# Ten column orders for the moving weights of the second MLP matrix, put back by VectorE

## The chip, the cores and the metric

One core of one Trainium2 chip runs the whole program. The metric is the device time of that core in microseconds (us), from the first to the last instruction of one execution; the lower the better. Two timed runs of the kernel before took 2423.46 and 2424.36 us, median 2423.91 us.

## The reference, cut to what matters

The program is one decoder layer over 512 tokens with a model width of 2048. What the change touches is the last matrix product, the second matrix of a squared-ReLU MLP with a hidden width of 8192:

```python
h = rmsnorm(x, g_mlp[l])
u = jnp.square(jax.nn.relu(jnp.einsum('bsd,df->bsf', h, w_ff1[l])))
x = x + jnp.einsum('bsf,fd->bsd', u, w_ff2[l])
return rmsnorm(x, g_final)
```

Here `u` is 512 x 8192, `w_ff2` is 8192 x 2048 and the result is 512 x 2048, all float32.

## The kernel before, in words

Every large product of the program is done by a scheme with seven block products in place of eight (Strassen's, in Winograd's form: A11, A12, S1 to S4, A22 name the seven left operands), and each float32 operand is split into a high and a low part of a rounded float32 format (`th` and `tl` on the weight side). A block product is then three matmuls for each slice of 128 of the inner dimension: high times high (line 187), high times low of the left operand (line 189), and the low part of the weights (line 191). ScalarE makes the high part (`high_of`, line 111), VectorE the low part (`low_of`, line 114).

The second MLP matrix is the loop at the end of the program. It runs over 8 segments of 1024 hidden columns (`seg`) and, in each, over two halves of 1024 output columns (`cg`): 16 **units**, each a call of `unit(seg, cg, ST)`. A unit loads four weight tiles `y` of 128 x 4 x 512 (line 1600, from the SP queue), forms three sums of them on VectorE (line 128), and runs its products through `run`, which splits the weights and calls `mm_rows`. There the stationary operand is a 128 x 128 piece of the left operand (`us`), and **the moving operand is a row slice `hi[:, q, :]` or `lo[:, q, :]` of the weights, 512 columns wide**, read from the first column to the last. One product is 2 row blocks x 12 matmuls of 512 columns. A unit has seven: four go to the PSUM accumulator `a` (A11, S2, S1, S4), two to the second accumulator `d` (S3, A22), one to `b` (A12).

After most products `into(i, j, ps)` adds the accumulator, two blocks of 128 x 512, onto the result rows `x` in SBUF: in the first segment ScalarE copies (line 1617), later VectorE adds (`add`, line 131), and where the residual has already been added to the rows (`in_rows`), VectorE multiplies by a factor for each row and adds (`onto_rows`, line 1535). The function `residual` (line 1578) puts one of the four places into `in_rows` at the end of each unit of segments 3 to 6: (0, 0), (1, 0), (1, 1), (0, 1) in that order. S3 goes to place (1, 1), A22 to place (1, 0).

The order of the work on each engine follows from the program's order and a scheduler that may move instructions; `a` and `d` swap their two PSUM bank pairs from unit to unit, so the `d` of one unit is the `a` of the next.

Of the kernel before, what the change touches and what calls it, by code (L numbers as in the profile page):

```python
# [11 lines left out]
AF = mybir.ActivationFunctionType  # L12
ALU = mybir.AluOpType
# [32 lines left out]
def tile_hybrid_block(ctx: ExitStack, tc, x, g_mix, w_in, b_f, b_gate, conv_w, w_conv_out,  # L46
                      w_attn_out, w_mix_out, g_mlp, w_ff1, w_ff2, g_final, out):
    nc = tc.nc
    x, out = x[0], out[0]
# [13 lines left out]
    def bank(i, name):  # L63
        return psum.tile([P, S], F32, tag=f"p{i}", name=name)
# [39 lines left out]
    def tied(i):  # L104

        if strict[0]:
            tc.keep_in_program_order(i)
        return i
# [7 lines left out]
    def split(src, hi, lo):  # L116
        return high_of(src, hi), low_of(src, hi, lo)
# [12 lines left out]
    def add(out, a, b):  # L130
        return nc.vector.tensor_tensor(out=out, in0=a, in1=b, op=ALU.add)
# [39 lines left out]
                    else:  # L171
                        nc.tensor.matmul(o, lo[:, q, js], Sh, start=False, stop=q == nq - 1, skip_group_check=True)  # L172

    def mm_rows(ps, Sx, hi, lo, first, extra=None, blocks=range(2), qs=None):

        nq, w = hi.shape[1], hi.shape[2]
        for b in blocks:
            o = ps[b][:, :w] if len(ps) == 2 else ps[0][:, b * w:(b + 1) * w]
            begin = first and (b == 0 or len(ps) == 2)
            ts = slice(b * P, (b + 1) * P)  # L180
            for part in range(2):
                for q in qs or range(nq):
                    Sh, Sl = (e[:, ts] for e in Sx(q))
                    if extra == "first" and part == 0 and q == 0 and b == 0:
                        nc.tensor.matmul(o[:, :192], Sh, hi[:, q, :192], start=True, stop=False, skip_group_check=True)
                    if part == 0:
                        tied(nc.tensor.matmul(o, Sh, hi[:, q, :], start=begin and q == 0, stop=False,  # L187
                                              skip_group_check=True))
                        tied(nc.tensor.matmul(o, Sl, hi[:, q, :], start=False, stop=False, skip_group_check=True))  # L189
                    else:  # L190
                        tied(nc.tensor.matmul(o, Sh, lo[:, q, :], start=False, stop=q == nq - 1,  # L191
                                              skip_group_check=True))

    def mm_late(ps, Sx, hi, lo, first):
# [331 lines left out]
    class Quarters:  # L526
# [28 lines left out]
        def turn(self, t, par, banks):  # L555

            out = []
            for n, i in enumerate(banks):
                pt = bank(i, "ptr").rearrange("p (k s) -> p k s", k=4)
                for k in range(4):  # L560
                    c = 2 * (4 * n + k) + par
                    tied(nc.tensor.matmul(pt[:, k, :], xin[t][:, c * P:(c + 1) * P], dgs[t], start=True, stop=True))
                out.append(pt)
            return out
# [147 lines left out]
    awake, pv = bank(3, "awake"), bank(7, "pv")  # L712
# [27 lines left out]
    a, b = (gV0.acc(k)[0] for k in "ab")  # L740
# [5 lines left out]
    pv = bank(2, "pv")  # L746
# [93 lines left out]
    for t in range(NT):  # L840
# [3 lines left out]
                            op0=ALU.mult)  # L844
# [51 lines left out]
    begin = {(q, k): const.tile([P, 1], F32, name=f"begin{q}{k}") for q in range(CT // 2) for k in range(3)}  # L896
    for b in begin.values():
        nc.vector.memset(b, 1.0)
    seen = const.tile([P, 1], F32, name="seen")
# [45 lines left out]
    def apart(i, name="S4", row=4):  # L945

        spare = bank(i, "spare")

        def extra(q, Sh, h):
            if q == row:  # L950
                nc.tensor.matmul(spare[:, :192], h[:, :P], Sh[:, :192], start=True, stop=True)
        return {name: extra}
# [17 lines left out]
    n = 0  # L970
    for g in (4, 2, 0, 5, 3, 1):
# [8 lines left out]
        if n == NH // 2:  # L980
# [5 lines left out]
                    extra={} if n < NH // 2 else {"A11": "first", **apart(4, "S2", 0)}))  # L986
# [3 lines left out]
    for f in range(0, KT, 2):  # L990
# [7 lines left out]
        if n == 4 + CT:  # L998
# [5 lines left out]
            for i, raw in enumerate(araw):  # L1004
# [3 lines left out]
                    extra=apart(4, "S2", 0)))  # L1008
# [46 lines left out]
    class Products:  # L1055
# [9 lines left out]
        def place(self, k, units):  # L1065
            self.tile(main.tile([P, 4, 2, 2, HS], F32R, tag=f"t{k}", name="M"), units)
# [157 lines left out]
    n = turns[0] + 1  # L1224
# [174 lines left out]
    common, turned = const.tile([P, 1], F32, name="common"), const.tile([P, NT], F32, name="turned")  # L1399
# [127 lines left out]
    in_rows = set()  # L1527
# [54 lines left out]
    def banks2(i, name):  # L1582
        return tuple(pairs.tile([P, S], F32, tag=f"q{i}{e}", name=name) for e in range(2))

    def unit(seg, cg, ST):

        a, d = banks2(cg, "a"), banks2(1 - cg, "d")
        if seg == 0:  # L1590
            kept[cg] = banks2(2 + cg, "b")
        b = kept[cg]
        X, at = {}, {}
        end = seg == NSEG - 1 and cg == 1
        for i, j in ((0, 1), (1, 1), (0, 0), (1, 0)) if end else ((0, 0), (1, 0), (0, 1), (1, 1)):
            at[i, j] = free.pop(0)
            t = main.tile([P, 4, S], F32, tag=f"x{at[i, j]}", name=f"y{i}{j}")
            c = NW * cg + S * j
            src = w_ff2[seg * 1024:(seg + 1) * 1024, c:c + S].rearrange("(q two p) c -> two p q c", two=2, p=P)
            nc.sync.dma_start(out=t, in_=src[i])  # L1600
            X[i, j] = t

        def run(ps, n, src, first):
            hi, lo = parts([P, 4, S])
            split(src, hi, lo)
            mm_rows(ps, ST[n], hi, lo, first)

        last = seg == NSEG - 1
        begun = set()

        def into(i, j, ps, end=False):
            for e in range(2):
                xs = place(i, j, cg, e)[2]
                if last and end:
                    finish(i, j, cg, ps, e)
                elif seg == 0 and (i, j) not in begun:
                    nc.scalar.activation(out=xs, in_=ps[e], func=AF.Copy)
                elif (i, j, cg) in in_rows:
                    onto_rows(i, j, cg, ps, e)
                else:  # L1620
                    add(xs, ps[e], xs)
            begun.add((i, j))

        t2 = main.tile([P, 4, S], F32, tag="t0", name="t2")
        if end:


            one = const.tile([P, 1], F32, name="one")
            nc.vector.tensor_copy(one, turned[:, 0:1])
            sub(t2, X[1, 1], X[0, 1])  # L1630
            run(a, "A11", X[0, 0], True)
            onto_rows(0, 0, cg, a, 1)
            onto_rows(0, 0, cg, a, 0, one)
            nc.vector.memset(one, 1.0)
            run(d, "S3", t2, True)
            sub(X[0, 0], X[0, 1], X[0, 0])
            sub(X[0, 1], X[1, 1], X[0, 0])
            into(1, 1, d)
            run(a, "S2", X[0, 1], False)
            sub(X[0, 1], X[1, 0], X[0, 1])  # L1640
            into(1, 0, a)
            for t in (2, 3):
                gain(t, one)
            run(d, "A22", X[0, 1], False)
            into(1, 0, d, True)
            run(a, "S1", X[0, 0], False)
            into(1, 1, a, True)
            p4 = (main.tile([P, 4, S], F32R, tag="t0", name="th4"),
                  main.tile([P, 4, S], F32R, tag=f"x{at[0, 1]}", name="tl4"))
            split(X[1, 1], *p4)  # L1650
            for t in (2, 3):
                Final(t).all()
            p2 = parts([P, 4, S])
            split(X[1, 0], *p2)
            for t in (0, 1):
                gain(t, one)
            for e in range(2):
                mm_rows(b, ST["A12"], *p2, False, blocks=(e,))
                finish(0, 0, cg, b, e)
                mm_rows(a, ST["S4"], *p4, False, blocks=(e,))  # L1660
                finish(0, 1, cg, a, e)
                Final(e).all()
            return
        run(a, "A11", X[0, 0], True)
        sub(X[0, 0], X[0, 1], X[0, 0])
        into(0, 0, a)
        run(b, "A12", X[1, 0], seg == 0)
        if seg == 0 and cg == 0:
            load_sums(0, (2, 3), us0)
        if last:  # L1670
            into(0, 0, b, True)
        sub(t2, X[1, 1], X[0, 0])
        run(a, "S2", t2, False)
        sub(X[0, 1], X[1, 1], X[0, 1])
        sub(t2, X[1, 0], t2)
        free.append(at[1, 0])
        into(1, 0, a)
        run(d, "S3", X[0, 1], True)
        free.append(at[0, 1])
        into(1, 1, d)  # L1680
        run(a, "S1", X[0, 0], False)
        free.append(at[0, 0])
        into(1, 1, a, True)
        run(d, "A22", t2, False)
        into(1, 0, d, True)
        run(a, "S4", X[1, 1], False)
        free.append(at[1, 1])
        into(0, 1, a, True)
        if 3 <= seg < 7:
            residual(*((0, 0), (1, 0), (1, 1), (0, 1))[seg - 3], cg)  # L1690

    kept = {}
    for seg in range(NSEG):
        ST = us0
        if seg > 0:
            ST = {}
# [36 lines left out]
```

## Time and profile before

| what | value |
|---|---|
| timed runs | 2423.46 and 2424.36 us, median 2423.91 us |
| span of the profiled execution | 2423.6 us, 0.3 us under the median |
| granted TensorE clock, mean | 0.998 |
| TensorE matmuls, busy | 2401.9 us (99%), 17783 |
| VectorE, busy | 2041.3 us (84%), 1739 |
| ScalarE, busy | 1202.6 us (50%), 1230 |
| the second MLP matrix, first to last matmul | from 1801.5 us on, to 2412.6 us |

The profiled execution's own time is its span; nothing else of it is given apart. The profile's page gives busy times by engine, the chain of work that ended last, and groups of instructions by line. Questions put to the trace give the same by stretches of time (windows), by shape of the instruction, in order of time (timeline), and the waits. A matmul's recorded duration holds the time from its start to the end of its results, so consecutive matmuls overlap in the records: what one costs in a row of them is the distance from one start to the next.

### The profile page before, as it was taken

The page shows a single profiled execution, that of the slowest core. Times are in us where ns is not written, and L with a number is a line of the kernel's source. Part 1 is how long each engine was busy: PE and PEld are TensorE (multiplying, and loading weights), DVE is VectorE, ACT ScalarE, POOL GpSimd, SP SyncE. Part 2 cuts the span into 40 slices and gives each one's busy share as a digit, 9 for nine tenths or more (in the row PEclk, how much of TensorE's full clock was granted, in tenths as well). Part 3 has the DMA queues.
Part 4 walks back from the last instruction along what each step waited for, and adds up shares of the span by engine and source line. Part 5 has one row for each costly group of instructions (what it writes and reads, how often), then busy time and mean ns, then how long its engine had stood idle before and what let it go on. Part 6 is the DMA issues. An engine that isn't in the chain of part 4 may idle for free.

```text
span 2423.6 us, 41438 instructions
## 1 busy us (share of the span) xinstructions
PE 2401.9 (99%) x17783; PEld 2260.7 (93%) x17783; DVE 2041.3 (84%) x1739; ACT 1202.6 (50%) x1230; POOL 299.9 (12%) x480
## 2 busy tenths in 40 slices
PE   9999999999999999999999999999999999999998
PEld 9999899999999999899999999999998888888886
DVE  7887677788887878898989889898887888889898
ACT  7443434445545534355666566666664333333334
POOL 1110111111111111022300000000011001100000
PEclk9999999999999999999999999999999999999999
DMA  8665454464656755657855564655678567665662
GB/s 276 188 187 153 148 157 140 144 189 152 201 187 199 239 179 187 209 169 243 315 201 207 198 232 177 231 192 200 229 296 291 166 217 251 217 206 184 235 229 101
DMA packets 279847, 491.98 MB, mean 203 GB/s; under 512 B 11820, under 2 KB 191112, under 8 KB 279280
## 3 DMA queue, kind: packets, MB, share of 16 engines
q1 hardware_dynamic: 226384, 272.71, 35.7%
q0 software_dynamic: 52672, 215.57, 24.3%
q8 instruction: 139, 2.28, 0.4%
q10 hardware_dynamic: 608, 1.06, 0.1%
q14 instruction: 44, 0.36, 0.0%
HBM read 379.70 MB, written 109.07 MB: 202 GB/s over the span
## 4 chain that ended last, share of the span: by engine, by line
PE 86%; DVE 4%; issue 4%; DMA 3%; ACT 1%; POOL 1%; SPq 0%; DVEq 0%; POOLq 0%; ACTq 0%
PE a L168 6%; PE a L172 6%; PE a L170 6%; PE a L189 5%; PE a L187 5%; PE a L191 5%; PE d L168 5%; PE d L170 5%; PE d L172 5%; PE c L168 4%; PE c L170 4%; PE c L172 4%; PE d L191 3%; PE d L189 3%; PE d L187 3%
## 5 line engine op out<-in xcount | busy, mean ns | idle before, releaser
L111 ACT ACTIVATE th<-x 128x2048 fp32r<-128x2048 f32 (+1 forms) x280 | 537.0, 1918 | 503.7 <-DVE x L128 159.2
L114 DVE TENSOR_TENSOR tl<-x,th 128x2048 fp32r<-128x2048 f32 (+2 forms) x282 | 639.4, 2273 | 162.1 <-ACT th L111 150.5
L128 DVE TENSOR_TENSOR x<-x,x 128x2048 f32<-128x2048 f32 (+1 forms) x160 | 366.0, 2288 | 24.4 <-DMA x<-in_w_in_dram 18.9
L111 ACT ACTIVATE th<-y 128x2048 fp32r<-128x2048 f32 (+1 forms) x109 | 185.4, 1701 | 273.9 <-PE a L189 138.8
L114 DVE TENSOR_TENSOR tl<-y,th 128x2048 fp32r<-128x2048 f32 (+1 forms) x109 | 219.0, 2014 | 29.3 <-ACT th L111 28.9
L187 PE MATMUL a<-th,us 128*128 128x512 f32 x512 | 199.3, 389 | 0.4 <-ACT th L111 0.4
L189 PE MATMUL a<-th,us 128*128 128x512 f32 x512 | 199.2, 389 | 0.0
L170 PE MATMUL c<-S,th 128*128 128x256 f32 x848 | 196.4, 277 | 0.0
L168 PE MATMUL c<-S,th 128*128 128x256 f32 x848 | 196.3, 277 | 0.0
L168 PE MATMUL a<-S,th 128*128 128x256 f32 x784 | 181.1, 277 | 0.0
L170 PE MATMUL a<-S,th 128*128 128x256 f32 x784 | 180.7, 276 | 0.0
L170 PEld LDWEIGHTS c<-S,th 128*128 128x128 f32 x848 | 159.3, 188 | 0.2 <-issue 0.2
L168 PEld LDWEIGHTS c<-S,th 128*128 128x128 f32 x848 | 159.4, 188 | 0.0
L170 PEld LDWEIGHTS a<-S,th 128*128 128x128 f32 x784 | 147.3, 188 | 0.0
L168 PEld LDWEIGHTS a<-S,th 128*128 128x128 f32 x784 | 147.2, 188 | 0.0
L191 PE MATMUL a<-tl,us 128*128 128x512 f32 x512 | 136.9, 389 | 0.6 <-DVE tl L114 0.6
L170 PE MATMUL b<-A,th 128*128 128x256 f32 x544 | 127.3, 279 | 0.0
L168 PE MATMUL a<-A,th 128*128 128x256 f32 x544 | 126.7, 278 | 0.0
L168 PE MATMUL d<-S,th 128*128 128x256 f32 x544 | 126.1, 277 | 0.0
L170 PE MATMUL a<-A,th 128*128 128x256 f32 x544 | 126.0, 277 | 0.0
L168 PE MATMUL b<-A,th 128*128 128x256 f32 x544 | 126.0, 276 | 0.0
L170 PE MATMUL d<-S,th 128*128 128x256 f32 x544 | 125.7, 277 | 0.0
(398 smaller groups left out, 6065.2 us busy)
## 6 DMA issues: line engine op xcount, KB each, us to landing
x<-in_w_in_dram SPq DMA_DIRECT2D x86, 1024.0 KB, 6.0
y<-in_w_ff_dram SPq DMA_DIRECT2D x64, 1024.0 KB, 7.7
x<-in_w_ff_dram SPq DMA_DIRECT2D x60, 1024.0 KB, 8.6
us<-s_d POOLq DMA_DIRECT2D x48, 1024.0 KB, 9.3
s_d<-rh POOLq DMA_DIRECT2D x32, 896.0 KB, 5.2
s_d<-r POOLq DMA_DIRECT2D x32, 896.0 KB, 6.0
x<-in_w_mix_out_dram SPq DMA_DIRECT2D x17, 1024.0 KB, 6.7
g_d<-o POOLq DMA_DIRECT2D x32, 256.0 KB, 3.1
```

What stands on the lines that cost most here:

```text
L111: return tied(nc.scalar.activation(out=hi, in_=src, func=AF.Copy))
L114: return tied(nc.vector.tensor_tensor(out=lo, in0=src, in1=hi.bitcast(F32), op=ALU.subtract))
L128: return nc.vector.tensor_tensor(out=out, in0=a, in1=b, op=ALU.subtract)
L168: nc.tensor.matmul(o, hi[:, q, js], Sh, start=first and q == 0 and j == 0, stop=False, skip_group_check=True)
L170: nc.tensor.matmul(o, hi[:, q, js], Sl, start=False, stop=False, skip_group_check=True)
L172: nc.tensor.matmul(o, lo[:, q, js], Sh, start=False, stop=q == nq - 1, skip_group_check=True)
L187: tied(nc.tensor.matmul(o, Sh, hi[:, q, :], start=begin and q == 0, stop=False, skip_group_check=True))
L189: tied(nc.tensor.matmul(o, Sl, hi[:, q, :], start=False, stop=False, skip_group_check=True))
L191: tied(nc.tensor.matmul(o, Sh, lo[:, q, :], start=False, stop=q == nq - 1, skip_group_check=True))
```

## The change

`mm_rows` gets an argument `seen`, a view that is laid on the weight slice before it is handed to the matmul as moving operand. In ten of the sixteen units the products that go to `d` (S3 and A22) use one of ten views, which read the same 512 columns in another order. The accumulator `d` then holds its columns in that order, and `into` reads it through the inverse view, so that the result rows are what they were. The products that go to `a` and `b`, the loads, the splits and the sums are as before. Units (0, 0) and (0, 1) and those of segments 6 and 7 keep the plain order.

| unit (seg, cg) | view | order in which the columns are read |
|---|---|---|
| (1, 0) | `runs(16, 2)` | runs of 16, alternately from 2 halves |
| (1, 1) | `runs(2, 2)` | runs of 2, alternately from 2 halves |
| (2, 0) | `runs(32, 4)` | runs of 32, in turn from 4 quarters |
| (2, 1) | `scattered(2)` | every 2nd column, then the others |
| (3, 0) | `swapped(16)` | neighbouring runs of 16 exchanged |
| (3, 1) | `backward()` | from the last column to the first |
| (4, 0) | `runs(8, 2)` | runs of 8, alternately from 2 halves |
| (4, 1) | `scattered(16)` | every 16th column, 16 times |
| (5, 0) | `swapped(2)` | neighbouring pairs exchanged |
| (5, 1) | `runs(64, 8)` | 8 runs of 64, one from each eighth (the plain order, since 8 x 64 = 512) |

A result view with four dimensions (`runs`, `swapped`) is added in one instruction with `add`; where the place is in `in_rows`, the loop over `m` makes one instruction for each piece: two of 256 columns in unit (5, 0), eight of 64 in unit (5, 1), for each block.

```diff
-    def mm_rows(ps, Sx, hi, lo, first, extra=None, blocks=range(2), qs=None):
+    def mm_rows(ps, Sx, hi, lo, first, extra=None, blocks=range(2), qs=None, seen=lambda t: t):
...
-                        tied(nc.tensor.matmul(o, Sh, hi[:, q, :], start=begin and q == 0, stop=False,
+                        tied(nc.tensor.matmul(o, Sh, seen(hi[:, q, :]), start=begin and q == 0, stop=False,
                                               skip_group_check=True))
-                        tied(nc.tensor.matmul(o, Sl, hi[:, q, :], start=False, stop=False, skip_group_check=True))
+                        tied(nc.tensor.matmul(o, Sl, seen(hi[:, q, :]), start=False, stop=False, skip_group_check=True))
                     else:
-                        tied(nc.tensor.matmul(o, Sh, lo[:, q, :], start=False, stop=q == nq - 1,
+                        tied(nc.tensor.matmul(o, Sh, seen(lo[:, q, :]), start=False, stop=q == nq - 1,
                                               skip_group_check=True))
...
+    def runs(n, m):
+
+        def read(t):
+            return t.rearrange("p (m o i) -> p o m i", m=m, i=n)
+
+        def back(t):
+            return t.rearrange("p (o m i) -> p m o i", m=m, i=n)
+
+        return read, back, lambda t: t.rearrange("p (m o i) -> p m o i", m=m, i=n)
+
+    def scattered(step):
+
+        return (lambda t: t.rearrange("p (a b) -> p b a", b=step), lambda t: t.rearrange("p (b a) -> p a b", b=step),
+                lambda t: t.rearrange("p (a b) -> p a b", b=step))
+
+    def swapped(n):
+
+        def turn(t):
+            return t.rearrange("p (o m i) -> p o m i", m=2, i=n)[:, :, ::-1, :]
+
+        return (turn, lambda t: turn(t).rearrange("p o m i -> p m o i"),
+                lambda t: t.rearrange("p (o m i) -> p m o i", m=2, i=n))
+
+    def backward():
+
+        return (lambda t: t[:, ::-1],) * 2 + (lambda t: t,)
+
+    ORDERS = {(1, 0): runs(16, 2), (1, 1): runs(2, 2), (2, 0): runs(32, 4), (2, 1): scattered(2), (3, 0): swapped(16),
+              (3, 1): backward(), (4, 0): runs(8, 2), (4, 1): scattered(16), (5, 0): swapped(2), (5, 1): runs(64, 8)}
+    plain = (lambda t: t,) * 3
...
-            mm_rows(ps, ST[n], hi, lo, first)
+            mm_rows(ps, ST[n], hi, lo, first, seen=order[0] if ps is d else lambda t: t)
...
+        order = ORDERS.get((seg, cg), plain)
+
         def into(i, j, ps, end=False):
+            if ps is d and order is not plain:
+                for e in range(2):
+                    xs = order[2](place(i, j, cg, e)[2])
+                    pv = order[1](ps[e])
+                    if seg == 0 and (i, j) not in begun:
+                        nc.scalar.activation(out=xs, in_=pv, func=AF.Copy)
+                    elif (i, j, cg) in in_rows:
+                        t = 2 * i + e
+                        for m in range(pv.shape[1]) if len(pv.shape) == 4 else (slice(None),):
+                            nc.vector.scalar_tensor_tensor(out=xs[:, m], in0=pv[:, m], scalar=turned[:, t:t + 1],
+                                                           in1=xs[:, m], op0=ALU.mult, op1=ALU.add)
+                    else:
+                        add(xs, pv, xs)
+                begun.add((i, j))
+                return
             for e in range(2):
                 xs = place(i, j, cg, e)[2]
                 if last and end:
```

How VectorE's program stands before and after at the place with the most pieces, the `into` of A22 in unit (5, 1) and what follows it at the start of unit (6, 0) (`x` are the result rows, `d` and `a` the accumulators, `turned` the factor by row, `y` and `t` the weight tiles and their sums, `tl` the low parts). Before:

```order
L114 TENSOR_TENSOR tl<-y_22436,th 128x2048
L1535 SCALAR_TENSOR_TENSOR x_19856<-d,turned,x_19856 128x512 x2
L114 TENSOR_TENSOR tl<-y_22671,th 128x2048
L131 TENSOR_TENSOR x_19855<-a,x_19855 128x512
L128 TENSOR_TENSOR y_22671<-y_22675,y_22671 128x2048
L131 TENSOR_TENSOR x_19855<-a,x_19855 128x512
L114 TENSOR_TENSOR tl<-y_22673,th 128x2048
L1535 SCALAR_TENSOR_TENSOR x_19855<-a,turned,x_19855 128x512
L128 TENSOR_TENSOR t_22679<-y_22677,y_22671 128x2048
L1535 SCALAR_TENSOR_TENSOR x_19855<-a,turned,x_19855 128x512
```

After:

```order
L114 TENSOR_TENSOR tl<-y_22438,th 128x2048
L1654 SCALAR_TENSOR_TENSOR x_19856<-d,turned,x_19856 128x64 x16
L114 TENSOR_TENSOR tl<-y_22687,th 128x2048
L131 TENSOR_TENSOR x_19855<-a,x_19855 128x512
L128 TENSOR_TENSOR y_22687<-y_22691,y_22687 128x2048
L131 TENSOR_TENSOR x_19855<-a,x_19855 128x512
L114 TENSOR_TENSOR tl<-y_22689,th 128x2048
L1535 SCALAR_TENSOR_TENSOR x_19855<-a,turned,x_19855 128x512 x2
L128 TENSOR_TENSOR t_22695<-y_22693,y_22687 128x2048
```

Sixteen pieces of 64 columns stand where two instructions of 512 stood, and in unit (6, 0) the sum `t` that S2 needs comes behind both additions of A11 instead of between them.

On TensorE the shapes and the order are the same throughout but for one place, the product S2 of unit (6, 0) (`a_22667` and `a_22668` before, `a_22683` and `a_22684` after, are the two row blocks of the accumulator). Before:

```order
L187 MATMUL a_22667<-th_22740,us_22658 128x512
L189 MATMUL a_22667<-th_22740,us_22658 128x512
L191 MATMUL a_22667<-tl_22741,us_22658 128x512 x4
L187 MATMUL a_22668<-th_22740,us_22658 128x512
L189 MATMUL a_22668<-th_22740,us_22658 128x512
```

After:

```order
L187 MATMUL a_22683<-th_22756,us_22674 128x512
L189 MATMUL a_22683<-th_22756,us_22674 128x512
L187 MATMUL a_22684<-th_22756,us_22674 128x512
L189 MATMUL a_22684<-th_22756,us_22674 128x512
L191 MATMUL a_22683<-tl_22757,us_22674 128x512 x4
```

Two matmuls of the second block, which need only the high part, stand ahead of the first block's four that need the low part. The instructions of ScalarE, GpSimd and SP keep their order.

## The prediction

> **What bounds the kernel now.** I began with the engines' busy times and the chain of work that ended last, then looked at the second MLP matrix alone, by windows of one unit each.
>
> ```profile
> PE 2401.9 (99%) x17783; PEld 2260.7 (93%) x17783; DVE 2041.3 (84%) x1739; ACT 1202.6 (50%) x1230; POOL 299.9 (12%) x480
> 1878.20:1916.28 38.08, 38.08 (x169) 31.53 (x169) 31.23 (x22) 14.11 (x9) 1.50 (x2) 1.00 0.60 195
> 2182.90:2220.90 38.00, 38.00 (x169) 31.49 (x168) 34.09 (x26) 13.45 (x7) 2.90 (x4) 1.00 0.65 218
> 2259.00:2297.10 38.10, 38.10 (x169) 31.55 (x169) 32.77 (x24) 13.45 (x7) 1.49 (x2) 1.00 0.60 200
> ```
>
> After the window and its length come PE, weight loads, DVE, ACT and POOL, then the granted clock. TensorE is busy for the whole of each window at a clock of 1.00, and the waits of TensorE between 1878 and 2373 us are an empty list. A busy matmul row could still hide gaps, so I checked the distance between starts and the chain:
>
> ```profile
> 2260.20 1.07 PE L191 MATMUL a<-tl,us 128*128 128x512 f32 x4
> 2262.91 1.07 PE L191 MATMUL a<-tl,us 128*128 128x512 f32 x4
> 2265.64 1.07 PE L191 MATMUL a<-tl,us 128*128 128x512 f32 x4
> ...
> 2241.32 0.91 PE d L191 x4
> 2244.04 0.91 PE d L191 x4
> ```
>
> The first three rows are the timeline, the last two the chain. Every block of 12 matmuls takes 2.72 us, so a matmul of 512 columns costs 226.7 ns and a unit of 168 of them 38.08 us: the windows to the last digit. This stage has no slack on TensorE. What a `d` matmul takes longer is paid in full, and what VectorE takes longer is paid only beyond its cover.
>
> Is the 226.7 ns a fixed cost plus columns, or columns alone?
>
> ```profile
> L951 PE MATMUL spare<-S,th 128*128 128x192 f32 x25 | 6.4, 257 | 0.0
> L172 PE MATMUL d<-S,tl 128*128 128x256 f32 x544 | 68.6, 277 | 0.0
> L187 PE MATMUL d<-th,us 128*128 128x512 f32 x256 | 99.7, 390 | 0.1
> L189 PE MATMUL d<-th,us 128*128 128x512 f32 x256 | 99.6, 389 | 0.0
> L191 PE MATMUL d<-tl,us 128*128 128x512 f32 x256 | 68.6, 390 | 0.6 <-DVE tl L114 0.6
> 1799.82 1.98 PE L172 MATMUL d<-A,tl 128*128 128x256 f32 x16
> ```
>
> Sixteen matmuls of 256 columns take 1.98 us; less the last one's 277 ns, 15 starts lie 113.5 ns apart, half of 226.7. So there is no fixed part: 0.443 ns for each column. A column that is slower to fetch therefore has no fixed time to hide in.
>
> **What the change costs, TensorE.** The three `d` rows hold 768 matmuls in 16 units, 48 in each. A unit's `d` matmuls cost 48 x 226.7 ns = 10.88 us. Unit (5, 1) reads 8 runs of 64 one behind the other, which is the plain order; nine units read otherwise. No moving operand in this trace is read in steps, so the price has to be bounded. Below: nothing, if a column is fetched for 0.443 ns wherever it lies. A gain is excluded, since the same 512 columns go through the same array, which these rows never show under 0.443 ns a column. Above, the nearest rows are the matmuls in full float32 and VectorE's reads:
>
> ```profile
> L869 PE MATMUL sc<-kT,qT 128*128 128x512 f32 x16 | 8.6, 622 | 0.6 <-DVE m L873 0.6
> L869 PE MATMUL sc<-kT,qT 128*128 128x128 f32 x16 | 3.4, 292 | 0.9 <-issue 0.6 <-DMA qT<-kq_d 0.2
> L131 DVE TENSOR_TENSOR x<-d,x 128x512 f32<-128x512 f32 x40 | 27.5, 688 | 26.4 <-PE d L191 26.4
> L131 DVE TENSOR_TENSOR r<-o,r 128x256 f32<-128x256 f32 x32 | 13.4, 419 | 0.0
> ```
>
> The first two give (622 - 292) / 384 = 0.86 ns a column, about double; VectorE moves one for (688 - 419) / 256 = 1.05 ns. By these, a unit whose columns are fetched one by one would pay 512 x 48 x 0.42 = 10.2 us or 512 x 48 x 0.61 = 14.9 us more.
>
> I choose a third reading. If TensorE were limited by its array, I would expect a fixed part at each matmul; a time that is columns alone looks like a stream that its memory feeds just fast enough. I assume that this memory hands over neighbours in groups, and that a group costs the same whether all of it is used or one column. Its width no row shows; with a group of four columns it costs 4 x 0.443 = 1.77 ns, and I take that. Then:
>
> - Runs of 8, 16 or 32 and exchanged runs of 16 use whole groups: units (1, 0), (2, 0), (3, 0), (4, 0) cost nothing more. Backward (3, 1) and exchanged pairs (5, 0) use all four columns of a group one behind the other: nothing, if the group is held.
> - Runs of 2 from two halves (1, 1) and every 2nd column (2, 1) use half of a group each time: double, 2 x 10.88 = 21.76 us more.
> - Every 16th column (4, 1) uses one of four: fourfold, 3 x 10.88 = 32.64 us more.
>
> The sum is 54.40 us; the price of (4, 1) goes beyond both bounds from other rows, and by the dearer of these (14.9 us for each of three units) the sum would be 44.7 us.
>
> [...]
>
> **What the change costs, VectorE.** Its `d` additions read PSUM in steps: 4 instructions a unit, 688 ns each. Were every column to cost double, that is 4 x 512 x 1.05 = 2.2 us a unit; the busiest plain window above has 38.00 - 34.09 = 3.9 us free. Taken at nothing; without that cover up to 2.2 us for each of nine units, 20 us. In unit (5, 1), 2 instructions become 16 of 64 columns, in (5, 0) 2 become 4:
>
> ```profile
> L1535 DVE SCALAR_TENSOR_TENSOR x<-d,turned,x 128x512 f32<-128x512 f32 x20 | 15.0, 748 | 7.7 <-PE d L191 7.7
> L876 DVE SCALAR_TENSOR_TENSOR bias<-m,cn 128x1 f32<-128x1 f32 x32 | 6.6, 216 | 0.6
> 2254.02 0.74 DVE L1535 SCALAR_TENSOR_TENSOR x<-d,turned,x 128x512 f32<-128x512 f32 x1
> 2255.86 0.75 DVE L1535 SCALAR_TENSOR_TENSOR x<-d,turned,x 128x512 f32<-128x512 f32 x1 [1.10 <-PE d L191]
> 2256.91 2.29 DVE L114 TENSOR_TENSOR tl<-y,th 128x2048 fp32r<-128x2048 f32 x1 [0.29 <-ACT th L111]
> 2271.98 0.39 PE L187 MATMUL a<-th,us 128*128 128x512 f32 x1
> 2273.80 1.07 PE L191 MATMUL a<-tl,us 128*128 128x512 f32 x4
> ```
>
> A piece of 64 costs 216 + 63 x 1.05 = 282 ns, 16 of them 4.5 us against 1.5: 3.0 us more, of which 1.10 + 0.29 us fall into VectorE's own waits. Behind them stands `tl` for A11 of unit (6, 0), due at 2262.91 us; it moves from 2256.91 to about 2258.5 and ends by 2261. Then the reordered program puts S2's sum `t` behind the second addition of A11, which has to wait for that block's last matmul at 2266.7. Then `t` ends near 2269.6, its high part at 2271.6 (wanted at 2271.98) and its low part near 2274.1, where 2273.80 was the need; the two matmuls moved ahead of it make that 2274.25. Taken at nothing, at most 1 us. Loads and queues are not touched.
>
> **The sum.** 54.40 + 0 on the profiled span of 2423.6 gives 2478.0; the median lies 0.3 us above that span, so **2478.3 us**. Two per cent, about what a measurement of this kernel tells from no change, is 48.5 us.
>
> **The rivals.**
>
> - *Two neighbours are enough* (chance 0.30). Only the stepping by 16 pays, 10.88 us at double up to 32.64 at fourfold; with the middle, 2423.9 + 21.8 = 2445.7. For it: the nearest rows from other instructions, 0.86 and 1.05 ns a column, are about double and not fourfold. Against: at 0.443 ns for every column the stream shows no spare time. [...]
> - *Any order but the plain one pays* (0.13): the stream is fast only for neighbours in rising order, and each of nine units pays double, 97.9 us: 2521.8. For it: nothing in the trace is fast in another form. Against: runs of 32 leave the row of neighbours only 16 times in 512 columns.
> - *Not slower* (0.14): the array's pace, not the fetch, is the 0.443 ns, and columns come one by one from wherever they lie. The `d` matmuls stay at 226.7 ns, VectorE hides in its 3.9 us, and the time is 2424. This decides as long as a fetch takes under 0.443 ns. For it: the time per column is the same at 192, 256 and 512. That the views did nothing would look the same; but the additions' shapes change, so they are there.
> - *VectorE becomes the bound* is worked out above: 20 us at most, small beside the rest (within the other cases' ranges).
>
> The forecast holds 0.43. Its own range is 2467 (one of the double orders free) to 2500 (backward and exchanged pairs double too, 21.8 more). The range reaches down to the free case and leaves out the dearest rival: **2423 to 2502**. Slower by over 2% (beyond 2472.4): 0.13 of the dearest and four fifths of the forecast's 0.43 make 0.47; within 2% 0.52; faster 0.01, taken from the third rival for what I do not see.
>
> **What would show it.** In the windows of the units, (2, 1) and (1, 1) near 49 us and (4, 1) near 70.7, the others at 38.1. The `d` rows should split into starts 227, 453 and 907 ns apart. If (4, 1) alone is long, the first rival is right; if all nine are near 49, the second; if none, the third. A TensorE wait for `tl` in unit (6, 0) would prove the cover wrong. A granted clock under 1.00 in the slow units would mean that I had missed a cause.

## The result, and the profile after

The changed kernel takes 2452.64 us (median of 2451.31 and 2453.98) against 2423.91 us: 28.7 us more. The ratio on record is 1.0114 with a 95% interval of 1.0085 to 1.0143 (the two medians alone give 1.0119). The forecast was 2478.3 us in a range of 2423 to 2502. The direction and the range held; of the forecast 54.4 us a little over half came. That the range held says little, since it reaches from no change to beyond the forecast.

The span of the profiled execution grew from 2423.6 to 2452.1 us, 28.5 us. The first line of the page's engine times shows where:

```profile
PE 2430.9 (99%) x17783; PEld 2263.2 (92%) x17783; DVE 2043.4 (83%) x1755; ACT 1202.2 (49%) x1230; POOL 300.0 (12%) x480
```

TensorE has 29.0 us more of busy time in as many matmuls, VectorE only 2.1 us. Next, windows cut at the first matmul of each unit, with the instructions on the tile `d` alone: the window, its length, then the busy time and number of the `d` matmuls on TensorE (PE), their weight loads, and the additions on VectorE (DVE). ScalarE's share (0 here), the granted clock, the busy share of the DMA engines and their GB/s close the row. The first row is a plain unit of the kernel before, (2, 1); the others are the changed kernel, from unit (1, 0) to (6, 0).

```profile
1994.54:2032.62 38.08, 11.20 (x48) 9.01 (x48) 2.75 (x4) 0.00 (x0) 1.00 0.68 232
1879.70:1918.52 38.82, 11.85 (x48) 9.14 (x48) 2.75 (x4) 0.00 (x0) 1.00 0.51 177
1918.52:1962.08 43.56, 16.63 (x48) 9.45 (x48) 2.77 (x4) 0.00 (x0) 1.00 0.63 220
1962.08:2000.56 38.48, 11.52 (x48) 9.05 (x48) 2.75 (x4) 0.00 (x0) 1.00 0.48 161
2000.56:2049.54 48.98, 22.07 (x48) 9.89 (x48) 2.77 (x4) 0.00 (x0) 1.00 0.57 195
2049.54:2087.98 38.44, 11.54 (x48) 9.04 (x48) 2.75 (x4) 0.00 (x0) 1.00 0.53 176
2087.98:2126.42 38.44, 11.54 (x48) 9.04 (x48) 2.75 (x4) 0.00 (x0) 1.00 0.68 249
2126.42:2165.32 38.90, 12.00 (x48) 9.14 (x48) 2.75 (x4) 0.00 (x0) 1.00 0.57 187
2165.32:2213.33 48.01, 21.12 (x48) 9.83 (x48) 2.77 (x4) 0.00 (x0) 1.00 0.58 197
2213.33:2251.41 38.08, 11.21 (x48) 9.01 (x48) 3.12 (x6) 0.00 (x0) 1.00 0.59 193
2251.41:2289.49 38.08, 11.21 (x48) 9.02 (x48) 4.62 (x18) 0.00 (x0) 1.00 0.68 247
2289.49:2327.60 38.11, 11.21 (x48) 9.02 (x48) 2.99 (x4) 0.00 (x0) 1.00 0.53 181
```

So a plain unit has 38.08 us and 11.20 us, and the price of an order is its TensorE time less 11.20, for 48 matmuls; divided by 48 and added to 226.7 ns it gives the time of one matmul.

| unit, order | forecast us | measured us | ns a matmul |
|---|---|---|---|
| (1, 0) runs of 16, 2 halves | 0 | 0.65 | 240 |
| (1, 1) runs of 2, 2 halves | 10.88 | 5.43 | 340 |
| (2, 0) runs of 32, 4 quarters | 0 | 0.32 | 233 |
| (2, 1) every 2nd | 10.88 | 10.87 | 453 |
| (3, 0) runs of 16 exchanged | 0 | 0.34 | 234 |
| (3, 1) backward | 0 | 0.34 | 234 |
| (4, 0) runs of 8, 2 halves | 0 | 0.80 | 243 |
| (4, 1) every 16th | 32.64 | 9.92 | 433 |
| (5, 0) pairs exchanged | 0 | 0.01 | 227 |
| (5, 1) plain | 0 | 0.01 | 227 |
| sum | 54.40 | 28.69 | |

The sum is the growth of the span to within 0.2 us, but in part by chance, since two differences ahead of these units nearly cancel. The loop began 1.9 us earlier than before (1799.76 against 1801.64 us): from 1098.30 to 1101.60 us the kernel before was granted a clock of 0.50 and the changed kernel 1.00, and half of that time, an estimate of 1.7 us, would account for most of it. Unit (0, 0) lasted 1.3 us longer than before (41.86 against 40.58). From the start of unit (1, 0) to the start of (6, 1) the time grew by 29.0 us. The granted clock is 1.00 in every row, and TensorE waits for nothing between 1878 and 2400 us: the list of its waits there is empty, as it was before.

### The profile page after: what moved, and what is told of

The parts are those of the page before. It is cut to its first block, busy times and chain, and to the rows that moved or that the text cites. A ratio compares the mean times of both kernels' runs of the same rounds, so it can differ in the third digit from the quotient of the medians.

```text
span 2452.1 us, 41453 instructions
## 1 busy us (share of the span) xinstructions
PE 2430.9 (99%) x17783; PEld 2263.2 (92%) x17783; DVE 2043.4 (83%) x1755; ACT 1202.2 (49%) x1230; POOL 300.0 (12%) x480
## 4 chain that ended last, share of the span: by engine, by line
PE 45%; DVE 2%; DMA 1%; ACT 1%; issue 1%; POOL 0%; DVEq 0%; POOLq 0%; ACTq 0%
PE a L189 4%; PE a L187 4%; PE a L191 4%; PE a L168 3%; PE a L170 3%; PE a L172 3%; PE d L191 3%; PE d L187 3%; PE d L189 3%; PE d L170 2%; PE d L168 2%; PE d L172 2%; PE b L189 1%; PE c L168 1%; PE b L170 1%; PE b L191 1%
## 5 line engine op out<-in xcount | busy, mean ns | idle before, releaser
L111 ACT ACTIVATE th<-t 128x2048 fp32r<-128x2048 f32 x31 | 59.5, 1919 | 141.0 <-DVE t L128 75.7
L168 PE MATMUL d<-S,th 128*128 128x256 f32 x544 | 126.0, 278 | 0.0
```

The lines of the kernel that those rows point to most:

```text
L111: return tied(nc.scalar.activation(out=hi, in_=src, func=AF.Copy))
L168: nc.tensor.matmul(o, hi[:, q, js], Sh, start=first and q == 0 and j == 0, stop=False, skip_group_check=True)
```

## The experiments

**TensorE's part and VectorE's part, each alone.** The first kernel keeps the reading orders and drops the inverse views, the second the reverse:

```diff
+    ORDERS = {k: (v[0],) + (lambda t: t,) * 2 for k, v in ORDERS.items()}
```

> Left out: VectorE does not put the columns back, so the result rows of the nine units stand in the order read; TensorE's ten orders are as in the change. Theory (the fetch of the moving columns): all of the 28.5 us comes from the matmuls, so 2452.5 within 1.5 us, and the d blocks of the units keep their starts (240, 340, 233, 452, 233, 233, 243, 432, 227 ns). Rival (VectorE's reading of PSUM in steps holds up TensorE's writing or its next product): near 2424, and the d matmuls near 227 ns.

```diff
+    ORDERS = {k: (lambda t: t,) + v[1:] for k, v in ORDERS.items()}
```

> Left out: TensorE reads the columns in the plain order, while VectorE still adds through the ten inverse views, so the result rows of the nine units are permuted. Theory: 2424 within 1.5 us, VectorE's additions hide behind 38.08 us of TensorE a unit. Rival (VectorE's part is what costs): near 2452.

TensorE alone: 2454.45 us, ratio 1.0123 (1.0106 to 1.0140); its profiled span is 2451.7 us, and its `d` blocks have the starts of the change. VectorE alone: 2424.28 us, ratio 1.0001 (0.9992 to 1.0010). The whole cost is in the reading on TensorE; the views on VectorE's side, the sixteen pieces included, cost nothing that can be measured.

**Steps.** Eight units read every 2nd to every 256th column:

```diff
+    ORDERS = {(1, 0): 2, (1, 1): 4, (2, 0): 8, (2, 1): 16, (3, 0): 32, (3, 1): 64, (4, 0): 128, (4, 1): 256}
+    ORDERS = {k: (scattered(v)[0],) + (lambda t: t,) * 2 for k, v in ORDERS.items()}
```

> Left out: VectorE does not put the columns back. Eight units read every 2nd, 4th, 8th, 16th, 32nd, 64th, 128th and 256th column, in that order of units from (1, 0) to (4, 1). Theory (pairs of neighbours are fetched together, a lone column pays for a pair, and it does not matter where the next one lies): all eight between 425 and 460 ns a matmul, each unit 9.5 to 11.2 us longer, in all 76 to 90 us: 2500 to 2514. Rival 1 (a group of four as predicted, with every 16th column an exception that its distance makes cheap): every 4th and 8th near 907 ns, 32 us each for these, 2545 or more. Rival 2 (the distance decides, by a bank or line that is still busy): the eight spread by over 100 ns.

It took 2492.08 us, ratio 1.0278 (1.0257 to 1.0298). The same windows as above, units (1, 0) to (4, 1):

```profile
1880.49:1929.48 48.99, 22.07 (x48) 9.88 (x48) 2.76 (x4) 0.00 (x0) 1.00 0.44 139
1929.48:1978.85 49.37, 22.41 (x48) 9.89 (x48) 2.77 (x4) 0.00 (x0) 1.00 0.57 193
1978.85:2026.79 47.94, 21.02 (x48) 9.83 (x48) 2.77 (x4) 0.00 (x0) 1.00 0.39 131
2026.79:2074.80 48.01, 21.12 (x48) 9.81 (x48) 2.76 (x4) 0.00 (x0) 1.00 0.57 198
2074.80:2122.89 48.09, 21.20 (x48) 9.83 (x48) 2.77 (x4) 0.00 (x0) 1.00 0.42 142
2122.89:2173.67 50.78, 23.86 (x48) 9.92 (x48) 2.76 (x4) 0.00 (x0) 1.00 0.58 198
2173.67:2214.43 40.76, 13.86 (x48) 9.19 (x48) 2.77 (x4) 0.00 (x0) 1.00 0.50 166
2214.43:2252.03 37.60, 10.68 (x48) 9.06 (x48) 2.75 (x4) 0.00 (x0) 1.00 0.67 234
```

Steps of 2 to 64 cost about double, 431 to 490 ns. A step never costs fourfold, so the forecast's reading of a group of four falls as it stood. But a step of 128 costs 282 ns, and a step of 256 is **faster than the plain order**: 10.68 us in place of 11.20, 216 ns a matmul. The theory that a column without a neighbour pays for a pair falls with these two rows: in a step of 256 (0, 256, 1, 257, ...) no two columns that follow one another are neighbours. The other rival, the distance, foretold a spread of over 100 ns, and it is there; but the price does not follow the distance (431, 435, 490, 282 and 216 ns for steps of 8, 32, 64, 128 and 256), and no row shows a bank or line that is still busy.

**Runs and hops.** Runs of 2, 4 and 8 from more and nearer places:

```diff
+    ORDERS = {(1, 0): (2, 2), (1, 1): (2, 4), (2, 0): (2, 8), (2, 1): (2, 16), (3, 0): (2, 32), (3, 1): (2, 64),
+              (4, 0): (2, 128), (4, 1): (4, 2), (5, 0): (4, 8), (5, 1): (4, 32), (6, 0): (8, 8), (6, 1): (8, 32)}
+    ORDERS = {k: (runs(*v)[0],) + (lambda t: t,) * 2 for k, v in ORDERS.items()}
```

> Left out: VectorE does not put the columns back. Runs of 2 from 2, 4, 8, 16, 32, 64 and 128 places in turn (hops of 1024 down to 16 bytes, units (1, 0) to (4, 0)), runs of 4 from 2, 8 and 32 places ((4, 1), (5, 0), (5, 1)), runs of 8 from 8 and 32 places ((6, 0), (6, 1)). Theory (a hop costs one column's time wherever it goes): runs of 2 all near 340 ns, runs of 4 near 283, runs of 8 near 253 or below; in all about 47 us: 2471. Rival (the distance of the hop decides): runs of 2 that hop 64 bytes or less near 227 to 260 ns and only the far ones at 340, in all 20 to 30 us: 2444 to 2454. Rival 2 (a hop costs only where a fetch of four is cut): runs of 4 and 8 at 227 whatever the hop.

It took 2501.82 us, ratio 1.0318 (1.0297 to 1.0339), 77 us over the kernel before and far over both expectations. Runs of 2 from 2, 8 and 128 places, and runs of 4 from 2 and 32 places:

```profile
1879.74:1923.30 43.56, 16.63 (x48) 9.45 (x48) 2.77 (x4) 0.00 (x0) 1.00 0.47 157
1971.94:2022.72 50.78, 23.86 (x48) 9.92 (x48) 2.77 (x4) 0.00 (x0) 1.00 0.37 123
2169.06:2218.05 48.99, 22.07 (x48) 9.88 (x48) 2.77 (x4) 0.00 (x0) 1.00 0.42 137
2218.05:2257.36 39.31, 12.35 (x48) 9.06 (x48) 2.75 (x4) 0.00 (x0) 1.00 0.67 239
2297.97:2335.98 38.01, 11.09 (x48) 8.99 (x48) 2.87 (x4) 0.00 (x0) 1.00 0.68 247
```

A hop of 16 bytes (128 places, 453 ns) costs as much as the far ones, so the distance is not it; and 128 places cost the same 22.07 us as every 2nd column. Runs of 4 are between 224 and 278 ns. All three theories named before the run fall. What fits most rows of both kernels is another one. Deal the columns of an order out to two readers, one taking the 1st, 3rd, 5th, the other the 2nd, 4th, 6th. In a step of 256 each reader walks through neighbours; in the plain order each takes every other column; in every order at 431 to 490 ns, most runs of 2 among them, a reader never finds two columns of one group of four behind each other. In runs of 2 from 2 places (340 ns) and in the step of 128 (282 ns) it does not either, but there it goes to and fro between only two groups. What the theory does not tell is the spread of the runs of 4: each reader has two columns of a group there, as in the plain order, and they took 251, 278 and 224 ns.

One rival falls by the rows at hand: a single reader that keeps the last two groups. It would fetch a group for every two columns in the step of 2 and for every column in the step of 16, which were 453 and 433 ns; and runs of 2 from 2 places would be as cheap for it as the plain order, but took 340 ns against 227.

**Two readers.** The next kernel was made to test that: columns one by one in turn from `n` places that lie `a` columns apart.

```diff
+    def places(n, a):
+
+        return lambda t: t.rearrange("p (o b a) -> p o a b", b=n, a=a)
+    ORDERS = {(0, 0): (2, 2), (0, 1): (2, 4), (1, 0): (2, 8), (1, 1): (2, 16), (2, 0): (2, 32), (2, 1): (2, 64),
+              (3, 0): (2, 128), (3, 1): (2, 256), (4, 0): (4, 4), (4, 1): (4, 16), (5, 0): (4, 2), (5, 1): (8, 2),
+              (6, 0): (8, 8), (6, 1): (4, 64)}
```

> Left out: VectorE does not put the columns back. The columns are read one by one in turn from n places that lie a columns apart: (n, a) = (2, 2), (2, 4), (2, 8), (2, 16), (2, 32), (2, 64), (2, 128), (2, 256) in the units (0, 0) to (3, 1), then (4, 4), (4, 16), (4, 2), (8, 2), (8, 8), (4, 64) in (4, 0) to (6, 1). Theory (two readers: one fetches the 1st, 3rd, 5th column of the order, the other the 2nd, 4th, 6th; each fetches groups of four columns, and pays unless it uses two or more of a group one behind the other): (2, 4) to (2, 256) all near 216 ns, since each reader then uses all four, (2, 2) near 227 as the plain order, with two of four; (4, 4) and wider near 282, (4, 2) and (8, 2) over 280, (8, 8) near 490. Rival (one reader, and only places far apart are cheap to alternate): 216 ns only at (2, 256), and (2, 4) to (2, 64) between 282 and 460 like steps and runs of 2.

Its only run took 2456.14 us, beside 2425.82 us for the kernel before. First unit (0, 0) of the kernel before, then of this one, with two places 2 columns apart (two other matmuls on a tile `d` count in both); then units (0, 1), (1, 1), (3, 1) with two places 4, 16 and 256 columns apart, (4, 0) and (5, 0) with four places, (5, 1) and (6, 0) with eight:

```profile
1801.64:1842.22 40.58, 11.66 (x50) 8.93 (x48) 2.06 (x3) 1.16 (x2) 1.00 0.93 326
1798.66:1840.69 42.03, 11.71 (x50) 8.94 (x48) 2.06 (x3) 1.17 (x2) 1.00 0.90 321
1840.69:1878.34 37.65, 10.69 (x48) 9.08 (x48) 1.37 (x2) 1.17 (x2) 1.00 0.78 275
1916.75:1954.39 37.64, 10.69 (x48) 9.08 (x48) 2.75 (x4) 0.00 (x0) 1.00 0.67 237
2067.23:2104.83 37.60, 10.69 (x48) 9.08 (x48) 2.75 (x4) 0.00 (x0) 1.00 0.67 245
2104.83:2145.00 40.17, 13.21 (x48) 9.08 (x48) 2.75 (x4) 0.00 (x0) 1.00 0.58 190
2185.20:2228.76 43.56, 16.65 (x48) 9.43 (x48) 2.88 (x4) 0.00 (x0) 1.00 0.51 168
2228.76:2279.11 50.35, 23.38 (x48) 10.02 (x48) 2.88 (x4) 0.00 (x0) 1.00 0.58 200
2279.11:2327.07 47.96, 21.04 (x48) 9.84 (x48) 3.00 (x4) 0.00 (x0) 1.00 0.40 130
```

All seven distances from 4 to 256 columns stand at 216 ns, as foretold (256 was known from the steps), though the columns themselves are out of order in seven ways; 2 columns apart stays near the plain order, 228 against 227. The one-reader rival, which allowed 216 only at 256, falls. Four places cost 268 (near the 282 named) and 340, eight places 480; (8, 8) was named near 490 and took 432. In the orders of four places each reader goes to and fro between two groups; why that costs from 268 to 340 ns is open.

**Where a group begins.** The last of the measuring kernels lays the split weights some columns further along:

```diff
+            hi, lo = parts([P, 4, S], SHIFTED.get((seg, cg), (1, 512, 0))[2] if ps is d else 0)
```

> Left out: VectorE does not put the columns back. The split weights of the d products lie some columns (4 bytes each) behind the start of their buffer. Order (n, a) from n places a columns apart, @ offset: (2, 4)@0, plain@1, plain@2, (2, 4)@1, (2, 4)@2, (2, 4)@3, (2, 4)@4, (2, 2)@1, (2, 2)@2, (2, 2)@3, (2, 2)@4, (2, 256)@2, (2, 256)@1 in the units (0, 1) to (6, 1). Theory (each of the two readers takes groups of four columns that begin at multiples of 16 bytes): plain@1 and @2 227; (2, 4)@0 and @4 216, @2 near 227 (two and two), @1 and @3 dearer (three and one); (2, 2)@1, @2 and @4 near 227, @3 over 400 (every column alone); (2, 256) 216 to 218 at both. Rival (groups follow the order of reading and not the address): no offset changes anything. Rival 2 (groups of two at multiples of 8 bytes): (2, 2)@1 dearer than @2.

Its only run took 2428.88 us, beside 2425.14 us. Order (2, 4) at offsets 0, 1, 2, 3 and 4, in units (0, 1) and (2, 0) to (3, 1), then the plain order at offset 1, unit (1, 0), and order (2, 2) at offset 3, unit (5, 0):

```profile
1841.03:1878.67 37.64, 10.69 (x48) 9.07 (x48) 1.37 (x2) 1.17 (x2) 1.00 0.77 273
1955.75:1995.87 40.12, 13.13 (x48) 9.20 (x48) 2.75 (x4) 0.00 (x0) 1.00 0.50 165
1995.87:2034.06 38.19, 11.23 (x48) 9.01 (x48) 2.75 (x4) 0.00 (x0) 1.00 0.67 236
2034.06:2074.12 40.06, 13.14 (x48) 9.16 (x48) 2.75 (x4) 0.00 (x0) 1.00 0.56 182
2074.12:2111.76 37.64, 10.69 (x48) 9.06 (x48) 2.75 (x4) 0.00 (x0) 1.00 0.67 244
1878.67:1917.31 38.64, 11.72 (x48) 9.10 (x48) 2.75 (x4) 0.00 (x0) 1.00 0.53 180
2188.59:2226.87 38.28, 11.35 (x48) 9.06 (x48) 2.87 (x4) 0.00 (x0) 1.00 0.62 208
```

216, 267, 227, 267 and 216 ns: four columns of a group, then three and one, two and two, one and three, and four again. So, by this theory, the groups are four columns of 4 bytes and begin at multiples of 16 bytes, counted from the start of the buffer. Order (2, 256) stayed at 217 ns at offsets 1 and 2, as foretold. Order (2, 2) at offset 3, named over 400, took 230. That was my slip and not the theory's: its first reader takes 3, 4, 7, 8, and 4 and 7 lie in one group. Something else is left over: the plain order took 238 and 233 ns at offsets 1 and 2 instead of 227, and (2, 2) at offset 1 also 238. At offset 4, a whole group, (2, 2) took 232. An offset has a small price of its own, which the theory does not tell. Groups of two would have made (2, 2) at offset 1 dearer too; but the plain order pays the same there, and groups of two do not tell 216 from 227.

**A version that beats both kernels.** Two places for all products of the second MLP matrix, with everything computed; VectorE and ScalarE read the accumulator through the inverse view:

```diff
+    def halves(t):
+
+        return t.rearrange("p (b a) -> p a b", b=2)
...
-            mm_rows(ps, ST[n], hi, lo, first)
+            mm_rows(ps, ST[n], hi, lo, first, seen=halves)
...
-                    add(xs, ps[e], xs)
+                    add(rows(xs), back(ps[e]), rows(xs))
```

> All work done. Every product of all 16 units reads the weights one column from each half in turn (the order that took 216 ns in place of 227), and VectorE and ScalarE put the columns back as they read the accumulator. Theory (paid and saved in full on TensorE): 16 x 168 x 10.9 ns = 29.3 us less, 2395 us, a unit 36.25 us. Rival (VectorE, 33 to 34 us busy in a plain unit, becomes the bound or is late with a low part): a unit between 36.5 and 38 us, 2400 to 2424, with TensorE waits for VectorE in the trace.

2405.74 us, ratio 0.9917 (0.9900 to 0.9933): faster by 0.8%, by 19.4 us of span in place of the 29.3 expected. Units (0, 1) to (1, 1) and (6, 0), and TensorE's waits from 1800 us on:

```profile
1841.79:1878.05 36.26, 10.69 (x48) 9.07 (x48) 1.38 (x2) 1.18 (x2) 1.00 0.80 290
1878.05:1916.58 38.53, 10.69 (x48) 9.07 (x48) 2.75 (x4) 0.00 (x0) 1.00 0.54 180
1916.58:1952.84 36.26, 10.69 (x48) 9.07 (x48) 2.75 (x4) 0.00 (x0) 1.00 0.66 244
2244.47:2281.82 37.35, 10.69 (x48) 8.99 (x48) 2.99 (x4) 0.00 (x0) 1.00 0.59 198
```

```profile
PE a L187 <- ACT th L111: 3.4, 3, 2.6
PE b L191 <- DVE tl L114: 1.6, 1, 1.6
PE d L187 <- ACT th L111: 1.1, 1, 1.1
PE a L191 <- DVE tl L114: 0.8, 1, 0.8
PE d L191 <- DVE tl L114: 0.3, 1, 0.3
```

Both expectations hold in part: undisturbed units last 36.26 us as worked out, others wait for a high part from ScalarE or a low part from VectorE that comes late, 7.2 us in this list against 1.6 before. The cover that hid VectorE at 38.08 us a unit is used up in these units. Right behind the longest wait, 2.57 us up to 1813.61 us, the granted clock was 0.50 from 1813.55 to 1816.95 us, and matmuls started 427 ns apart; the rows shown have 1.00. From 1795 us on, the distances between matmul starts that are over a tenth too long add up to 13.0 us above 216 ns each, against 2.7 us above 227 ns before. These 10.3 us more cover the 9.9 us that did not come.

The same order in nearly every large product of the program:

```diff
-                        nc.tensor.matmul(o, hi[:, q, js], Sh, start=first and q == 0 and j == 0, stop=False,
+                        nc.tensor.matmul(o, hi[:, q, js], halves(Sh), start=first and q == 0 and j == 0, stop=False,
...
-                pairs = [(s[:, b, :], ps[b][:, :self.w]) for b in range(2)]
+                pairs = [(s[:, b, :].rearrange("p (b a) -> p b a", b=2),
+                          ps[b][:, :self.w].rearrange("p (a b) -> p b a", b=2)) for b in range(2)]
```

> All work done. The order that read one column from each half in turn is used in nearly every large product of the program (256 columns wide in the earlier stages), and ScalarE and VectorE put the columns back as they read the accumulators. [...] Rival (the halves of a 256-column row are too near, or the left operands stored in the other phases hinder it): 113 ns a matmul, 2400 to 2406.

2386.26 us, ratio 0.9834 (0.9817 to 0.9850), the fastest here, and below the 2400 to 2406 that a matmul of still 113 ns would give. Had the order saved the same share of a 256-column matmul as of one of 512 (10.9 of 226.7 ns), 113.3 ns would have become about 108 and some 13800 of them would have saved 75 us, down to about 2330: an estimate, and the result fell between the two. Two rows of its timeline, in a stage with 256 columns:

```profile
1399.76 0.83 PE L176 MATMUL a<-S,tl 128*128 128x256 f32 x6
1400.43 0.28 PE L172 MATMUL d<-A,th 128*128 128x256 f32 x1
```

Six matmuls from 1399.76 to 1400.43 us are 111.7 ns each, against 113.3 before and the 108 of the estimate. Some 13800 of them save 1.6 ns each, 22 us at most, and that is about what came on top (2405.7 to 2386.3, 19 us). Matmuls of 260 columns stand at the same 112 ns, so at this width it is no longer the columns that set the pace. What does was not tried. A candidate is the weight load that each matmul has of its own: from 1300 to 1400 us the loads are busy for all of the 100 us, 898 beside 898 matmuls, while in the second MLP matrix they are busy for 70 of 80 us (1900 to 1980). They were busy throughout in the kernel before too (100 us of the same 100, 884 beside 885 matmuls), so this alone does not settle it.

## Why the prediction was right, and where its terms were wrong

- *No slack on TensorE, paid in full.* Right: 28.69 us of longer `d` matmuls, 28.5 us of span.
- *48 matmuls and 10.88 us a unit; unit (5, 1) plain.* Right.
- *VectorE at nothing.* Right. The `d` additions keep their time in every view (0.69 us; 4 of them 2.75 us a unit before and after). The sixteen pieces of unit (5, 1) took 4.62 - 1.38 = 3.24 us with the other two additions taken off, about 203 ns each, since their records (275 ns) overlap. The prediction's 282 ns a piece, 4.5 us together, was too dear by 1.3 us, on the safe side; units (5, 1) and (6, 0) last 38.08 and 38.11 us: the narrow times worked out for S2's low part left no wait.

```profile
L1654 DVE SCALAR_TENSOR_TENSOR x<-d,turned,x 128x64 f32<-128x64 f32 x16 | 3.2, 275 | 0.2 <-PE d L191 0.2
L1654 DVE SCALAR_TENSOR_TENSOR x<-d,turned,x 128x256 f32<-128x256 f32 x4 | 1.7, 478 | 1.0 <-PE d L191 1.0
L131 DVE TENSOR_TENSOR x<-d,x 128x512 f32<-128x512 f32 x40 | 27.6, 689 | 54.6 <-PE d L191 54.6
```

- *The step that failed: "Every 16th column (4, 1) uses one of four: fourfold, 3 x 10.88 = 32.64 us more."* It measured 9.92. No row of before showed the width of four, and no run shows a fourfold price: the dearest order of all took 490 ns, 2.2 times the plain one. The width was right, as the offsets showed; that one reader takes the groups one after the other was not. If there are two readers, a column alone costs 433 / 256 = 1.7 ns of its reader, near the 1.77 ns worked out, but two such fetches run side by side. This term alone is 22.7 of the 25.7 us by which the sum was too high.
- *Runs of 2 at double.* 5.43 instead of 10.88: half. Each reader goes to and fro between the same two groups, which costs less (340 ns) than four or more groups in turn (431 to 490). Why is open.
- *Every 2nd column at double.* 10.87 against 10.88, by luck: the prediction let one reader use two columns of a group, by the two readers each takes one column of every group, and both come to double.
- *Whole groups free.* Nearly: 0.3 to 0.8 us for five orders, 2.5 us together, which the forecast put at nothing; pairs exchanged cost 0.01.
- *"A gain is excluded."* Wrong as a rule, though no order of the change gained: 216 ns for two places against 227. The rows of before showed only one order, and a bound over orders cannot be read from one.
- *A time that is columns alone as the sign of a stream fed just fast enough.* It pointed the right way: the plain order can be read faster in another order, by 11 of its 227 ns. That a limit of the array would show as a fixed part was my assumption; no run shows it.
- *The rivals.* The first gave 2445.7 us, nearer than the forecast, but its mechanism, that only the step of 16 pays, is refuted by unit (2, 1), which paid more (10.87 us against 9.92), and runs of 2, free by it, took 340 to 490 ns. Counted for each of the two readers, two neighbours were not quite enough either: two of a group took 227 ns in the plain order, four took 216. The dear rival falls with six orders other than the plain one at 227 to 243 ns, and "not slower" with the result.

That there are two readers is inferred from times and not shown otherwise. Named beforehand, the six new distances at 216 ns came, and so did two columns apart near 227 and the pattern of (2, 4) over five offsets. It missed (8, 8) by 58 ns, and the plain order and (2, 2) at some offsets by 5 to 11 ns. The spread between 431 and 490 ns among orders of lone columns is not explained, nor that between 224 and 278 ns among the runs of 4.

## What to carry to other kernels

Where a matmul of this float32 format is limited by its moving operand, look at the order as if dealt out to two readers: each should use two, better four, columns of a 16-byte group one behind the other (here 227 and 216 ns for 512 columns, against 431 to 490 with one). Two interleaved streams, 4 to 256 columns apart and beginning at a multiple of 16 bytes, beat the plain order by 11 of 227 ns, and the view that puts the columns back cost VectorE nothing that could be measured. Before such a gain is booked, check what else sets the pace: here late high and low parts of the weights, with a stretch at half the clock behind the longest wait, took back a third of it (9.9 of 29.3 us), and at 256 columns a matmul fell by only 1.6 of 113.3 ns.

## What the runs showed of the hardware that I had not expected

- The times fit a moving read with two sides: 216 ns for 512 columns with four of a group for each reader, 227 with two in the plain order, 267 with three and one, 268 to 340 when each goes to and fro between two groups, 431 to 490 with one column of a group at a time.
- An address order that no neighbour follows (0, 256, 1, 257) is the fast one.
- VectorE's additions of 512 columns from PSUM took 682 to 693 ns in every view of the change, columns hopping by 1 KB included.
- A row of the plain order that begins 4 or 8 bytes behind the start of its buffer took 238 or 233 ns instead of 227.
